# A two-layer hybrid decoder trunk: the instruction order found with the compiler's other model of time

## The chip, the cores and the metric

The kernel runs on one core of one Trainium2 chip. The metric is the device time of one execution in microseconds (us). The engines are TensorE (PE in the profile; its weight loads are PEld), VectorE (DVE), ScalarE (ACT), GpSimd (POOL) and SyncE (SP), which issues most of the DMAs. Each engine takes its own instructions strictly in the order in which they stand in its program and waits on semaphores for the others.

## The reference

Two layers of a decoder trunk on one sequence of S = 512 tokens and width D = 1024, all in fp32. The core of it, shortened:

```python
def hybrid_layer(x, ...):
    proj = rmsnorm(x, norm1_g) @ w_in            # 1024 -> 9568 columns, split among the branches
    y_ssd = ssd_mixer(ssd_z, ssd_xbc, ssd_dt, ...)        # Mamba-2: causal conv, chunked scan, gated norm
    y_mla = mla_mixer(mla_cq, mla_ckv, mla_kr, ...)       # 8 heads of latent attention, causal softmax
    y_gdn = gdn_mixer(gdn_qkv, gdn_z, gdn_b, gdn_a, ...)  # gated DeltaNet: causal conv, chunked recurrence
    mixed = g_ssd * (y_ssd @ w_ssd_out) + g_mla * (y_mla @ w_mla_out) + g_gdn * (y_gdn @ w_gdn_out)
    h = x + mixed @ w_out
    return h + square(relu(rmsnorm(h, norm2_g) @ w_up)) @ w_down     # 1024 -> 4096 -> 1024
```

In the chunked recurrences of the SSD and the DeltaNet (GDN) branch a state is carried from one chunk of tokens to the next. A final RMSNorm ends the trunk.

## The kernel before

The kernel is one long straight program without loops on the chip. Nearly all of its time is dense products on TensorE. An fp32 product is made of three matmuls on halves of the operands (`xh`, `xl` of the activations, `whi`, `wlo` of the weights), each with 512 columns as a rule:

```python
198    x = pe.matmul(o, ah, bh, start=start, stop=False, skip_group_check=more)
201    pe.matmul(o, ah, bl, start=False, stop=False, skip_group_check=more)
202    return pe.matmul(o, al, bh, start=False, stop=stop, skip_group_check=more)
```

The weights arrive by DMA as raw fp32 (`wraw`, `wr`), ScalarE casts the high half (L170) and VectorE subtracts to get the low half (L171). The results of dense products go to four PSUM banks (`acc`); a product can begin only when the bank of the fourth product before it has been read out. Three further banks (`sm`) and one more (`yt`) serve the small steps.

A layer runs in this order: front projection; latent attention (MLA, L590 to L711) in four pairs of heads `hp`; two SSD groups (L740 to L848); the triangular inverses for GDN; two GDN units `u` (`gdn_unit`, L1006 to L1137); the branch output projections (`out_proj`, L493), gates, `w_out`; then the feed-forward part. Each branch consists of chains of small steps that pass from engine to engine. The program writes them interleaved with dense products of the same or of the next branch, so that TensorE has something to do while VectorE and ScalarE work on a chain.

Three chains matter here.

- **A GDN chunk** (four chunks `t` of 128 tokens in each unit): TensorE L1057 and L1068, VectorE L1071 (four slices), TensorE L1074, VectorE L1079, ScalarE L1085 (four slices), TensorE L1088, VectorE L1097 (four slices: the new state `st`, which the next chunk's L1068 needs). Beside it the chunk's output: TensorE L1100 and L1107, ScalarE L1108, VectorE L1110, ScalarE L1116, VectorE L1122 and L1123, the inverse root of L278 (VectorE) and L279 (POOL), VectorE L1125 and L1128. L1108 writes the buffer `wk3`, of which there is one, so it waits for the L1128 of the chunk before. After the last chunk the transposes L1133 take the unit's output to `yt`, L274 (ScalarE) and L275 (VectorE) split it into `yh`, `yl`, and these are operands of `w_gdn_out`.
- **An MLA head**: scores on TensorE (L667 to L671) for four blocks of rows, VectorE L676 (mask and maximum), ScalarE L678 (exponential), VectorE L679 and L680, then transposes on TensorE (L688), whose results ScalarE (L270) and VectorE (L271) split, then the products with the values (L704 to L706).
- **A causal convolution** of a dense result (`conv_silu`, L720): ScalarE L725, then three times VectorE L729, which read the `acc` bank; L283 finishes the SiLU.

The order on each engine is not the order of the text. The tile framework builds the program from the text, with buffers from pools and semaphores between the engines, and a list scheduler inside it chooses at each step among the instructions that are ready, by a model of what each costs. The text steers it in two ways: `tc.high_priority()` marks steps as urgent, and `behind(key, ins)` (L153) ties a small step to stand behind a chosen dense product, by a dependency that sets the order only and puts no semaphore into the program:

```python
151    tc.add_manual_dep(i, o.name, order_only, reason="behind a product")
1085   act.activation(hv(vd)[:, h], hv(pw)[:, h], AF.Copy, scale=cd[:, t, h : h + 1])
1110   dve.scalar_tensor_tensor(hv(o)[:, h], hv(pq)[:, h], hdec(0, t, h), hv(o)[:, h], ALU.mult, ALU.add)
```

## Time and profile before

| what | value |
|---|---|
| time, median of 2 runs | 2269.6 us (2269.21 to 2269.99) |
| profiled execution, device time | 2269.02 us |
| its span in the profile | 2267.2 us |
| mean granted TensorE clock | 0.999 |
| TensorE (PE) busy | 2251.3 us, 99% |
| VectorE (DVE) busy | 1649.1 us, 73% |
| ScalarE (ACT) busy | 1185.1 us, 52% |
| GpSimd (POOL) busy | 64.6 us, 3% |
| moved by DMA | 244.07 MB, mean 108 GB/s |

The span is counted from the first to the last instruction of the profiled execution; about 2 us of device time lie outside it. "Busy" counts the time in which an engine has at least one instruction under way. Matmuls are pipelined: the row of one shows a longer duration than the step from its start to the start of the next.

### The profile page before, as it was taken

The page shows a single profiled execution, that of the slowest core. Times are in us where ns is not written, and L with a number is a line of the kernel's source. Part 1 is how long each engine was busy: PE and PEld are TensorE (multiplying, and loading weights), DVE is VectorE, ACT ScalarE, POOL GpSimd, SP SyncE. Part 2 cuts the span into 40 slices and gives each one's busy share as a digit, 9 for nine tenths or more (in the row PEclk, how much of TensorE's full clock was granted, in tenths as well). Part 3 has the DMA queues.
Part 4 walks back from the last instruction along what each step waited for, and adds up shares of the span by engine and source line. Part 5 has one row for each costly group of instructions (what it writes and reads, how often), then busy time and mean ns, then how long its engine had stood idle before and what let it go on. Part 6 is the DMA issues. An engine that isn't in the chain of part 4 may idle for free.

```text
span 2267.2 us, 32128 instructions
## 1 busy us (share of the span) xinstructions
PE 2251.3 (99%) x11758; PEld 1868.3 (82%) x11758; DVE 1649.1 (73%) x3315; ACT 1185.1 (52%) x2444; POOL 64.6 (3%) x84
## 2 busy tenths in 40 slices
PE   9999999999999999999999999999999999999998
PEld 8888888888888888888888878888888888888886
DVE  8886567776767778767868865668657668778668
ACT  6665744333443555554656657443345445645545
POOL 1000000000000000000010000000001000000000
PEclk9999999999999999999999999999999999999999
DMA  4223633442225143233132246335422251433231
GB/s 143 82 78 109 194 104 119 137 135 75 84 65 177 56 149 112 94 111 103 52 101 80 71 125 192 103 111 149 122 84 75 66 186 38 167 112 102 84 112 47
DMA packets 220030, 244.07 MB, mean 108 GB/s; under 512 B 34256, under 2 KB 172384, under 8 KB 219872
## 3 DMA queue, kind: packets, MB, share of 16 engines
q1 hardware_dynamic: 219872, 242.02, 34.7%
q8 instruction: 92, 1.51, 0.3%
q14 instruction: 66, 0.54, 0.1%
HBM read 225.53 MB, written 11.74 MB: 105 GB/s over the span
## 4 chain that ended last, share of the span: by engine, by line
PE 95%; DVE 3%; DMA 1%; ACT 1%; POOL 0%; issue 0%; SPq 0%; DVEq 0%; POOLq 0%; ACTq 0%
PE acc L198 24%; PE acc L202 24%; PE acc L201 24%; PE sm L201 3%; PE sm L198 3%; PE sm L202 3%; PE sm L688 1%; PE sm L792 1%; DVE wlo L171 1%; PE yt L704 1%; PE sm L1074 1%; PE sm L1100 1%; PE sm L803 1%; PE yt L201 1%; PE yt L198 1%; PE yt L202 1%
## 5 line engine op out<-in xcount | busy, mean ns | idle before, releaser
L171 DVE TENSOR_TENSOR wlo<-wraw,whi 128x512 fp32r<-128x512 f32 (+1 forms) x536 | 364.9, 686 | 331.9 <-ACT whi L170 321.8
L170 ACT CAST whi<-wraw 128x512 fp32r<-128x512 f32 (+1 forms) x536 | 329.3, 618 | 518.8 <-PE acc L201 345.7
L198 PE MATMUL acc<-xh,whi 128*128 128x512 f32 (+1 forms) x1344 | 525.3, 391 | 0.0
L202 PE MATMUL acc<-xh,wlo 128*128 128x512 f32 (+1 forms) x1344 | 520.6, 388 | 0.6 <-DVE wlo L171 0.6
L201 PE MATMUL acc<-xl,whi 128*128 128x512 f32 (+1 forms) x1344 | 519.2, 387 | 0.0
L202 PEld LDWEIGHTS acc<-xh,wlo 128*128 128x128 f32 x1344 | 252.5, 188 | 50.4 <-DVE wlo L171 1.4
L198 PEld LDWEIGHTS acc<-xh,whi 128*128 128x128 f32 x1344 | 252.5, 188 | 48.2 <-ACT xh L274 0.4
L201 PEld LDWEIGHTS acc<-xl,whi 128*128 128x128 f32 x1344 | 252.7, 188 | 47.6 <-DVE xl L275 0.7
L170 ACT CAST whi<-wr 128x512 fp32r<-128x512 f32 x168 | 104.4, 621 | 109.5 <-PE acc L201 47.3
L198 PE MATMUL acc<-yh,whi 128*128 128x512 f32 x384 | 152.1, 400 | 0.0
L201 PE MATMUL acc<-yl,whi 128*128 128x512 f32 x384 | 150.3, 391 | 0.0
L202 PE MATMUL acc<-yh,wlo 128*128 128x512 f32 x384 | 149.8, 390 | 0.0
L171 DVE TENSOR_TENSOR wlo<-wr,whi 128x512 fp32r<-128x512 f32 x168 | 113.0, 686 | 36.4 <-ACT whi L170 35.4
L729 DVE SCALAR_TENSOR_TENSOR ckl<-acc,pc,ckl 128x511 f32<-128x511 f32 (+2 forms) x168 | 121.2, 743 | 19.2 <-ACT ckl L725 10.9
L198 PEld LDWEIGHTS acc<-yh,whi 128*128 128x128 f32 x384 | 71.5, 188 | 16.5 <-ACT yh L274 2.3
L202 PEld LDWEIGHTS acc<-yh,wlo 128*128 128x128 f32 x384 | 72.1, 188 | 15.0
L201 PEld LDWEIGHTS acc<-yl,whi 128*128 128x128 f32 x384 | 72.1, 188 | 14.2
L198 PE MATMUL acc<-whi,xh 128*128 128x512 f32 (+1 forms) x208 | 79.9, 384 | 1.2 <-DVE ckl L729 1.2
L202 PE MATMUL acc<-whi,xl 128*128 128x512 f32 (+1 forms) x208 | 79.3, 381 | 0.0
L201 PE MATMUL acc<-wlo,xh 128*128 128x512 f32 (+1 forms) x208 | 79.2, 381 | 0.0
L488 ACT ACTIVATE eE<-eE,cum 128x128 f32<-128x128 f32 x192 | 62.5, 390 | 29.3 <-DMA eE<-d_c 24.5
L1220 DVE TENSOR_TENSOR h<-h,acc 128x512 f32<-128x512 f32 x120 | 76.9, 679 | 0.0
(468 smaller groups left out, 4498.7 us busy)
## 6 DMA issues: line engine op xcount, KB each, us to landing
wraw<-in_w_in_dram SPq DMA_DIRECT2D x144, 512.0 KB, 3.6
wraw<-in_w_up_dram SPq DMA_DIRECT2D x64, 512.0 KB, 3.6
wr<-in_w_down_dram SPq DMA_DIRECT2D x32, 1024.0 KB, 5.1
eE<-d_c SPq DMA_DIRECT2D x48, 256.0 KB, 4.3
wraw<-in_w_mla_out_dram SPq DMA_DIRECT2D x16, 512.0 KB, 3.3
eE<-d_e SPq DMA_DIRECT2D x32, 256.0 KB, 3.0
wraw<-in_w_ssd_out_dram SPq DMA_DIRECT2D x16, 512.0 KB, 3.3
wraw<-in_w_gdn_out_dram SPq DMA_DIRECT2D x16, 512.0 KB, 3.4
```

What stands on the lines that cost most here:

```text
L170: act.copy(hi, raw)
L171: dve.tensor_tensor(lo, raw, f32(hi), ALU.subtract)
L198: x = pe.matmul(o, ah, bh, start=start, stop=False, skip_group_check=more)
L201: pe.matmul(o, ah, bl, start=False, stop=False, skip_group_check=more)
L202: return pe.matmul(o, al, bh, start=False, stop=stop, skip_group_check=more)
L488: act.activation(o[:, i], o[:, i], AF.Relu, scale=-1.0, bias=cum[:, t, h0 + i : h0 + i + 1])
L688: pe.transpose(ps[:, n : n + P], pn[t][:, kb * P : (kb + 1) * P], ident)
L704: pe.matmul(o, v_h, th[:, c : c + w], start=kb == 0, stop=False)
L729: dve.scalar_tensor_tensor(acc[:, d:], ps[:, : S - d], taps_[3 - d], acc[:, d:], ALU.mult, ALU.add)
L792: x = pe.matmul(py[64 * i : 64 * i + 64, c * P : (c + 1) * P], xd[:, t, h * 64 : (h + 1) * 64], e2[h // 4][:, h % 4, :], start=True, stop= ...
L803: pe.matmul(po[:, c * P : (c + 1) * P], st[:, c * P : (c + 1) * P], ctl[:, tok], start=True, stop=True)
L1220: dve.tensor_tensor(hs_, hs_, ps[t], op)
```

## The change

One argument where the tile framework is opened. The function that computes, and with it every instruction, stays as it is.

```diff
-    with tile.TileContext(nc) as tc:
+    with tile.TileContext(nc, schedule_with_timeline_sim=True) as tc:
         hybrid_kernel(tc, args, out)
```

With it, the list scheduler asks another model of time what an instruction costs and when it would be ready, so it chooses another order on the engines. The buffers, the dependencies and the rules of `behind` and `high_priority` are the same. On TensorE about two rows in three stand at another place than before, the farthest more than 150 rows away; on VectorE most of the moves are within 30 rows, on SyncE within 17; GpSimd's order is the same. Three places show what moved. The names in the rows are the program's buffers with their numbers: `acc` and `sm` and `yt` are PSUM banks, `xh`/`xl`, `yh`/`yl`, `whi`/`wlo` the halves of operands; a row stands for one matmul or, with "x4", for four of the same names.

**The end of GDN unit u=1 in the first layer, on TensorE.** The rows of before, from the L1074 of chunk t=2 (`sm_1458`) to the transposes L1133 after the last chunk:

```order
L1074 MATMUL sm_1458_6831<-tok_1357_6346,tok_999_4501 128x128 x4
L198 MATMUL acc_1492_6972<-xh6_31_160,whi_1501_7025 128x512
...
L202 MATMUL acc_1505_7045<-yh0_1150_5419,wlo_1509_7050 128x512
L1088 MATMUL sm_1461_6843<-wk2_1460_6838,kt_1353_6332 128x256
...
L1107 MATMUL sm_1465_6857<-st_1444_6776,ft_1333_6230 128x256
L198 MATMUL acc_1505_7045<-yh1_1151_5420,whi_1508_7049 128x512
...
L1068 MATMUL sm_1475_6894<-st_1462_6846,ft_965_4342 128x256
...
L1074 MATMUL sm_1476_6901<-tok_1357_6346,tok_999_4501 128x128 x4
L198 MATMUL acc_1505_7045<-yh3_1153_5422,whi_1510_7065 128x512
...
L1100 MATMUL sm_1478_6908<-wk1_1477_6906,eE_1472_6886 128x128 x4
...
L1107 MATMUL sm_1480_6914<-st_1462_6846,ft_1333_6230 128x256
...
L1133 MATMUL yt_1487_6943<-ct_0_75,tok_1358_6347 128x128 x4
```

The rows of the change at the same place:

```order
L202 MATMUL acc_1522_7131<-xh7_32_161,wlo_1532_7185 128x512
L1074 MATMUL sm_1458_6831<-tok_1357_6346,tok_999_4501 128x128 x4
L1088 MATMUL sm_1461_6843<-wk2_1460_6838,kt_1353_6332 128x256
...
L1088 MATMUL sm_1461_6843<-wk2_1460_6838,kt_1354_6333 128x256
...
L1107 MATMUL sm_1465_6857<-st_1444_6776,ft_1333_6230 128x256
...
L1068 MATMUL sm_1475_6894<-st_1462_6846,ft_965_4342 128x256
L1074 MATMUL sm_1476_6901<-tok_1357_6346,tok_999_4501 128x128 x4
L1100 MATMUL sm_1478_6908<-wk1_1477_6906,eE_1472_6886 128x128 x4
...
L1107 MATMUL sm_1480_6914<-st_1462_6846,ft_1333_6230 128x256
L1133 MATMUL yt_1487_6943<-ct_0_75,tok_1358_6347 128x128 x2
L198 MATMUL acc_1505_7045<-yh4_1154_5423,whi_1513_7083 128x512
```

Before, 60 dense matmuls (L198, L201, L202 on `acc_1492`, `acc_1505`, `acc_1506`, `acc_1521`, `acc_1522`) stand between the first row and the L1133; in the change there is none, the rows of the chain follow one another, and those dense products stand ahead of it or behind. The second layer has the same picture.

**The end of GDN unit u=0, on VectorE.** Before, from the L1097 that makes the last state (`st_1303`) to the convolutions of `acc_1377` and `acc_1378`, whose banks a later dense product waits for:

```order
L1097 SCALAR_TENSOR_TENSOR st_1303_6104<-st_1285_6034,dec_254_1091,sm_1302_6101 128x128 x4
...
L1071 SCALAR_TENSOR_TENSOR tok_1198_5604<-sm_1316_6152,ndec_255_1093,tok_1198_5604 128x128 x4
L283 SCALAR_TENSOR_TENSOR ft_1332_6229<-ft_1332_6229,ckl0_1346_6301 128x512
...
L729 SCALAR_TENSOR_TENSOR ckl0_1372_6419<-acc_1359_6348,pc_13_122,ckl0_1372_6419 128x511
...
L729 SCALAR_TENSOR_TENSOR ckl0_1372_6419<-acc_1359_6348,pc_13_122,ckl0_1372_6419 128x510
...
L1110 SCALAR_TENSOR_TENSOR wk3_1320_6171<-sm_1321_6172,dec_254_1091,wk3_1320_6171 128x128 x2
...
L1037 TENSOR_TENSOR tok_1357_6346<-sm_1373_6426,gork_996_4493 128x4x128
...
L729 SCALAR_TENSOR_TENSOR ckl0_1390_6517<-acc_1377_6446,pc_13_122,ckl0_1390_6517 128x511
L275 SCALAR_TENSOR_TENSOR yl0_1158_5427<-yt_1328_6201,pc_13_122,yh0_1150_5419 128x512
...
L729 SCALAR_TENSOR_TENSOR ckl0_1390_6517<-acc_1377_6446,pc_13_122,ckl0_1390_6517 128x509
```

The rows of the change:

```order
L1097 SCALAR_TENSOR_TENSOR st_1303_6104<-st_1285_6034,dec_254_1091,sm_1302_6101 128x128 x4
L1110 SCALAR_TENSOR_TENSOR wk3_1305_6114<-sm_1306_6115,dec_254_1091,wk3_1305_6114 128x128 x4
L1071 SCALAR_TENSOR_TENSOR tok_1198_5604<-sm_1316_6152,ndec_255_1093,tok_1198_5604 128x128 x4
L283 SCALAR_TENSOR_TENSOR ft_1332_6229<-ft_1332_6229,ckl0_1346_6301 128x512
...
L729 SCALAR_TENSOR_TENSOR ckl0_1372_6419<-acc_1359_6348,pc_13_122,ckl0_1372_6419 128x511
L729 SCALAR_TENSOR_TENSOR ckl1_1375_6433<-acc_1360_6349,pc_13_122,ckl1_1375_6433 128x511
...
L1110 SCALAR_TENSOR_TENSOR wk3_1320_6171<-sm_1321_6172,dec_254_1091,wk3_1320_6171 128x128 x4
L729 SCALAR_TENSOR_TENSOR ckl0_1390_6517<-acc_1377_6446,pc_13_122,ckl0_1390_6517 128x511
...
L729 SCALAR_TENSOR_TENSOR ckl1_1393_6531<-acc_1378_6447,pc_13_122,ckl1_1393_6531 128x511
...
L729 SCALAR_TENSOR_TENSOR ckl0_1390_6517<-acc_1377_6446,pc_13_122,ckl0_1390_6517 128x509
...
L1037 TENSOR_TENSOR tok_1357_6346<-sm_1373_6426,gork_996_4493 128x4x128
```

The L1097, L1110, L1071 of the last two chunks and the L729 of four convolutions now stand close together, without the weight splits (L171) that were between them. On TensorE the chain from the L1088 of `sm_1302` to the L1107 of `sm_1321` has 40 dense matmuls in it before and none in the change.

**The last MLA head of the first layer (hp=3), on TensorE.** Before, from the last score matmul (`sm_527`) over the transposes L688 to the products with the values (`yt_531`):

```order
L671 MATMUL sm_527_2132<-kph_121_571,qpl1_148_688 128x512
L688 MATMUL sm_532_2146<-ct_0_75,pn0_517_2100 128x128
L198 MATMUL acc_564_2287<-xh3_28_157,whi_568_2306 128x512
L201 MATMUL acc_564_2287<-xl3_36_165,whi_568_2306 128x512
L688 MATMUL sm_532_2146<-ct_0_75,pn1_521_2113 128x128
...
L688 MATMUL sm_532_2146<-ct_0_75,pn3_529_2139 128x128
...
L201 MATMUL acc_564_2287<-xl4_37_166,whi_571_2324 128x512
L704 MATMUL yt_531_2145<-mix_533_2151,cqh1_483_1955 128x512
L202 MATMUL acc_564_2287<-xh4_29_158,wlo_572_2325 128x512
...
L705 MATMUL yt_531_2145<-mix_534_2152,cqh1_483_1955 128x512
...
L202 MATMUL acc_564_2287<-xh5_30_159,wlo_572_2325 128x512
```

The rows of the change:

```order
L671 MATMUL sm_527_2132<-kph_121_571,qpl1_148_688 128x512
L688 MATMUL sm_532_2146<-ct_0_75,pn0_517_2100 128x128
...
L688 MATMUL sm_532_2146<-ct_0_75,pn3_529_2139 128x128
...
L688 MATMUL sm_538_2169<-ct_0_75,pn3_529_2139 128x128
L704 MATMUL yt_531_2145<-mix_533_2151,cqh1_483_1955 128x512
L705 MATMUL yt_531_2145<-mix_534_2152,cqh1_483_1955 128x512
...
L706 MATMUL yt_531_2145<-pt0_145_683,cql1_484_1956 128x256
L764 MATMUL sm_576_2363<-ct_0_75,tok_542_2190 128x128 x4
L764 MATMUL sm_578_2377<-ct_0_75,tok_542_2190 128x128 x4
L198 MATMUL acc_607_2556<-xh0_25_154,whi_610_2560 128x512
```

Before, dense matmuls of the SSD projections (`acc_563`, `acc_564`) stand among the transposes and the value products; in the change none do, and right behind the L764 transposes comes `acc_607`, whose bank is that of `acc_579`.

## The prediction

> **What bounds the kernel now.** I read the page's busy times first, then the chain that ended last, then TensorE's waits and its groups by shape.
>
> ```profile
> PE 2251.3 (99%) x11758; PEld 1868.3 (82%) x11758; DVE 1649.1 (73%) x3315; ACT 1185.1 (52%) x2444; POOL 64.6 (3%) x84
> PE 95%; DVE 3%; DMA 1%; ACT 1%; POOL 0%; issue 0%; SPq 0%; DVEq 0%; POOLq 0%; ACTq 0%
> PE sm L1068 <- ACT wk L1108: 1.2, 2, 0.6
> PE acc L198 <- DVE ckl L729: 1.2, 2, 0.6
> ```
>
> TensorE is busy for 2251.3 of 2267.2 us, the chain runs on it for 95% of the span, and its longest wait in the middle of the program is 0.6 us (waits: us in total, times, longest). Of the 15.9 us without a matmul about 9 lie after the last one and 1 at the head. So every other engine's time counts only where TensorE has to wait for it, and an order can only win what waiting is left.
>
> Some waiting hides in the busy time, because a matmul that is issued late shows as a longer row:
>
> ```profile
> L198 PE MATMUL acc<-xh,whi 128*128 128x512 f32 x1280 | 507.6, 397 | 0.0
> L202 PE MATMUL acc<-xh,wlo 128*128 128x512 f32 x1280 | 502.8, 393 | 0.6 <-DVE wlo L171 0.6
> L201 PE MATMUL acc<-xl,whi 128*128 128x512 f32 x1280 | 501.1, 391 | 0.0
> L198 PE MATMUL sm<-xh,whi 128*128 128x512 f32 x176 | 68.5, 389 | 0.0
> L198 PE MATMUL acc<-yh,whi 128*128 128x512 f32 x384 | 152.1, 400 | 0.0
> ```
>
> The undisturbed group has 389 ns. The excess is (8 + 4 + 2) x 1280 = 18 us, and for the L198 with `yh` 11 x 384 = 4 us. With the 6 us of listed waits and a few us in smaller groups, **about 30 us of waiting are in the kernel**, all that an ideal order could win. A gain of more than 2% (45 us, about what a measurement of this kernel can tell from no change) is then not to be had.
>
> **The change part by part.** No instruction is added or removed, so TensorE's work is the same and only waiting can differ. The order decides where the dense matmuls stand, and the question for each chain is how many stand inside it. I price each place as the length of the chain minus TensorE's own work in it.
>
> *(a) The end of GDN unit u=1.* Before, this stretch of the first layer costs nothing:
>
> ```profile
> 674.90:696.60 21.70, 21.70 (x118) 18.74 (x117) 15.74 (x54) 8.86 (x29) 3.02 (x3) 1.00 0.18 49
> 674.92 1.05 PE L1074 MATMUL sm<-tok,tok 128*128 128x128 f32 x8
> 676.01 0.69 DVE L1079 TENSOR_TENSOR wk<-sm,gcc 128x512 f32<-128x512 f32 x1
> 676.73 0.88 ACT L1085 ACTIVATE wk<-sm,gcd 128x128 f32<-128x128 f32 x3 [1.02 <-DVE wk L1079]
> 678.01 0.38 ACT L1085 ACTIVATE wk<-sm,gcd 128x128 f32<-128x128 f32 x1
> 679.89 1.11 DVE L1097 SCALAR_TENSOR_TENSOR st<-st,dec,sm 128x128 f32<-128x128 f32 x4
> 680.92 1.12 DVE L1110 SCALAR_TENSOR_TENSOR wk<-sm,dec,wk 128x128 f32<-128x128 f32 x4
> 683.75 1.12 DVE L1071 SCALAR_TENSOR_TENSOR tok<-sm,ndec,tok 128x128 f32<-128x128 f32 x4
> 686.88 1.05 PE L1100 MATMUL sm<-wk,eE 128*128 128x128 f32 x8
> 687.76 1.03 PE L1107 MATMUL sm<-st,ft 128*128 128x256 f32 x4
> 688.12 0.58 ACT L1108 COPY wk<-sm 128x512 f32<-128x512 f32 x1 [3.63 <-DVE tok L1128]
> 688.44 0.58 PE L198 MATMUL acc<-yh,whi 128*128 128x512 f32 x1
> 691.12 0.16 DVE L1122 TENSOR_TENSOR gms<-gos,grt 128x4 f32<-128x4 f32 x1 [0.20 <-ACT gk L1116]
> 691.76 1.01 POOL L279 TENSOR_TENSOR gms<-gms,nhalf 128x4 f32<-128x4 f32 x1 [5.12 <-DVE gms L278]
> 693.00 1.14 DVE L1128 SCALAR_TENSOR_TENSOR tok<-tok,gms,wk 128x128 f32<-128x128 f32 x4
> L1061 DVE TENSOR_TENSOR gk<-sm,ct 128x256 f32<-128x256 f32 x16 | 6.7, 416 | 0.0
> L1063 DVE TENSOR_TENSOR eE<-eE,gk 128x512 f32<-128x512 f32 x16 | 11.0, 687 | 0.0
> L1116 ACT ACTIVATE gk<-wk 128x128 f32<-128x128 f32 x64 | 19.1, 299 | 6.7 <-DVE wk L1110 6.5
> L274 ACT ACTIVATE yh<-yt,pc 128x512 fp32r<-128x512 f32 x16 | 11.0, 687 | 11.6 <-PE yt L1133 11.5
> ```
>
> The window has TensorE at 21.70 of 21.70 us (first pair of numbers; the 1.00 is the granted clock), since 60 dense matmuls stand in the chain and beside it. In the change none does. Then the chain from the end of the first L1074 runs at its own speed: L1079 0.69, L1085 1.26, the L1088 and L1100 behind them about 0.95 more, L1097 1.11, L1110 1.12 and L1071 1.12 in VectorE's order; then L1061, L1063 and two rows of 0.16 like L1122 (1.4), beside which the last L1074 runs; L1079 0.69, L278 0.17, L279 on POOL 1.01 with 0.2 of hand-over, L1125 0.16, L1128 1.14: 11.0 us. L1108 needs the one `wk3` that this L1128 reads (its row above names that wait), so the last chunk's output starts only now: L1108 0.58, L1110 1.12, the last L1116 0.5, L1122 to L278 0.5, L279 1.2, L1125 0.16, L1128 1.14: 5.2. With hand-overs 16.4 us until L1133. TensorE's work in it, by steps from start to start: eight of 128 columns take 0.88 (L1100 to L1107), 0.11 each, four of 256 columns 0.68 (L1107 to the L198), 0.17 each. An fp32 instruction counts two. L1074, L1100 twice and L1057 are 28 of the former, L1088, L1107 twice and L1068 are 16 of the latter: 3.1 + 2.7 = 5.8. The stall is 16.4 - 5.8 = 10.6 us, about 6 of it in one piece between the last L1107 and the L1133. Then comes `acc_1505` on `yh4`, which needs L1133 and ScalarE's 0.7 us L274, for four tiles in turn, partly covered: 2 us. So **12.5 us per layer, 25 in all**.
>
> *(b) The end of unit u=0.* The change has no dense matmul in the chain here either, and VectorE runs late with the convolutions.
>
> ```profile
> L729 DVE SCALAR_TENSOR_TENSOR ckl<-acc,pc,ckl 128x511 f32<-128x511 f32 (+2 forms) x168 | 121.2, 743 | 19.2 <-ACT ckl L725 10.9
> L283 DVE SCALAR_TENSOR_TENSOR ft<-ft,ckl 128x512 f32<-128x512 f32 x36 | 24.5, 686 | 1.7 <-ACT ft L282 1.3
> ```
>
> From the L1097 of `st_1303` to the L729 that frees the bank of `acc_1377` VectorE holds 10 to 12 L729 of 0.743 (8.2), five runs of four slices (L1097, L1110 twice, L1071, L1128: 5.6), four L283 (2.7), L1061, L1063, L1079 (1.8) and small rows (1.2): 19.5 us. TensorE has about 12.3 us until `acc_1397`, which needs that bank: the chain's 5.8, the 24 matmuls of `acc_1395` and `acc_1396` at 0.227, and 1 of transposes. The stall is **7.2 us per layer, 14 in all**.
>
> *(c) MLA.* Per head, the last score block needs L676 to L680 before its L688 can run, and the L688 need L270 and L271 before L704 and L705:
>
> ```profile
> L676 DVE CUSTOM_DVE_ANT_0 pn<-sm,causal,qrs 128x512 f32<-128x512 f32 x16 | 11.9, 743 | 0.6 <-PE sm L671 0.5
> L678 ACT ACTIVATE pn<-pn,mx 128x512 f32<-128x512 f32 x16 | 11.5, 720 | 1.1 <-DVE mx L676 0.9
> L679 DVE RECIPROCAL sme<-sme 128x1 f32<-128x1 f32 x64 | 10.1, 158 | 0.9 <-ACT pn L678 0.7
> L680 DVE TENSOR_SCALAR pn<-pn,sme 128x512 f32<-128x512 f32 x16 | 7.8, 485 | 0.4
> L271 DVE TENSOR_TENSOR mix<-sm,mix 128x512 fp32r<-128x512 f32 x16 | 11.0, 690 | 6.3 <-ACT mix L270 6.1
> L766 DVE TENSOR_TENSOR tok<-sm,dtq 128x512 f32<-128x512 f32 x16 | 10.4, 683 | 0.3 <-PE sm L764 0.3
> ```
>
> L676 0.74, L678 0.72, L679 0.16, L680 0.49 and an estimated 0.3 for the read-outs of the accumulators between them are 2.4; the L688 of the earlier blocks cover a few tenths: 2.2. L704 and L705 wait another 0.9, the rest of the L270 and L271 that the other transposes don't cover. 3.1 for each of the last two heads, in which the change has no dense matmul: 6.2. Then `acc_607` waits for the bank of `acc_579`: behind the last L706, L270 0.6, L271 0.69, two L766 1.37 and four L729 2.97 are 5.6, less 0.9 of transposes on TensorE, and L270 starts a little before the last L706: 4. Two us more for the earlier heads, which lose some of their matmuls. **12 us per layer, 24 in all.**
>
> *(d) What goes.* The waits that are there now, about 30 us, are replaced by those above at the same places, and in the SSD stage and the feed-forward part the change keeps two or more dense matmuls between small steps. I count them as gone: **-30 us**. Bounds: 0, if each stays, and -30.
>
> *(e) The clock.* The trace shows once what an idle TensorE does to it, at the end:
>
> ```profile
> 2258.00:2260.00 2.00, 0.24 (x2) 0.00 (x0) 1.81 (x5) 0.32 (x1) 0.01 (x1) 1.00 0.74 285
> 2260.00:2262.00 2.00, 0.00 (x0) 0.00 (x0) 1.43 (x3) 0.40 (x2) 0.54 (x1) 1.00 0.28 109
> 2262.00:2264.00 2.00, 0.00 (x0) 0.00 (x0) 1.24 (x4) 0.00 (x0) 0.55 (x1) 0.56 0.68 262
> 0.99 7.56 PE L352 MATMUL yt<-cosT 128*128 128x128 f32 x44 [0.99 <-POOL cosT L109]
> ```
>
> The last matmul ends at 2258.24; the granted clock is 1.00 up to 2262 and 0.56 on average in the two us behind: it halves 4.0 us after the last matmul. The 6 us piece of (a) is longer. The price of coming back is not in the trace; nearest is the first row of the program, 44 matmuls of 172 ns where the eight of L1100 take 0.88 us, 110 each: 2.7 us more. Between 0 and 2.7 per layer I take 2.5, as near to that row: **+5**.
>
> [...]
>
> *SyncE.* Two of the first weight loads are issued after some small loads, but they wait for buffers until about 10 us in both orders: 0. For the rest, weights are loaded and split further ahead than TensorE uses them (L171 costs it 0.6 us in all), and moves of 17 rows don't use that up.
>
> **The sum:** 25 + 14 + 24 - 30 + 5 = +38 us on the profiled 2269.0, which is 0.6 below the median of the runs: **2307 us, slower by 1.7%**.
>
> **Rivals.**
> - *The bare chains cost more (slower by over 2%).* The durations above are those of undisturbed steps. If VectorE is late at the start of each chain by one split (L171 0.69) per step, or the waits of (d) stay at their places, 10 to 30 us come on top: 2317 to 2340. For it: VectorE is 73% busy, and in (b) it is the bound. Against it: the change's rows put the splits ahead of the chains. 0.36.
> - *The chains are covered after all (faster than before).* The mechanism: the dense matmuls that the change puts ahead of a chain put TensorE behind VectorE there, so that the chain's steps are ready when TensorE arrives, and only the -30 us of (d) acts. It decides if the stalls of (a) to (c) together stay under 30 us, half of their 63. Time 2245 to 2267, for example 2255 with 15 us of stalls left. Against it: in (a) each step needs the one before it, so nothing can be ready ahead. 0.10.
> - *No effect.* Stalls of about 30 us that replace the 30 of before: 2267 to 2280. 0.10.
> - *My forecast*, 2280 to 2316: 0.44.
>
> **Range and chances.** Low end: half of (a) to (c) gone gives 2275, and a part of the case of no effect lies below that, so 2270; high end: none of the 30 us of (d) goes and VectorE is late besides, 2345. That leaves 0.10 out below and 0.08 above. Faster by over 2% needs 45 us, more than all waiting: 0.01. Slower by over 2% (above 2315) is the first rival and the edge of the forecast: 0.39. Within 2%: 0.60.
>
> **What would show it.** In the profile of the changed kernel the waits of TensorE should list L1133 after L1128 with two waits of 5 to 6 us, L1068, L1074 and L1100 of GDN with 1 to 3 us each, `acc` L198 after L729 with some 7 us in two of them, and L688 after L680 with some 2 us; TensorE's busy time should fall by about the hidden 25 us. A granted clock under 1.00 in the window behind the L1133 shows (e). The excess of the L198 `acc<-xh,whi` group over 389 ns should shrink. The prediction is wrong if TensorE's listed waits stay under 20 us, if the stalls stand at other places than these three, or if weights arrive late (L201 or L202 waiting for L170, L171 or a DMA).

## The result, and the profile after

The change makes the kernel slower: 2370.9 us, median of two runs (2370.32 and 2371.51), against 2269.6; ratio 1.0444, 95% interval 1.0427 to 1.0461. The profiled execution took 2370.32 us, its span is 2368.5: 101.3 us more than before. The prediction had the direction; its 2307 us and its range up to 2345 are too low.

The busy times on the page of the changed kernel:

```profile
PE 2283.0 (96%) x11758; PEld 1898.6 (80%) x11758; DVE 1650.5 (70%) x3315; ACT 1177.8 (50%) x2444; POOL 68.5 (3%) x84
```

The counts are those of before. TensorE idles for 2368.5 - 2283.0 = 85.5 us, before 15.9: **69.6 us more idle**. And the same number of matmuls, 11758, kept it busy for **31.7 us more**. These are two different losses, and they add up to the 101.3.

The first is in TensorE's list of waits (us in total, times, longest), which has 76.1 us in all and had 6.3:

```profile
PE yt L1133 <- DVE tok L1128: 10.1, 2, 5.1
PE acc L198 <- DVE ckl L729: 9.7, 3, 4.6
PE sm L754 <- DVE ft L283: 7.7, 2, 4.2
PE sm L688 <- DVE pn L680: 7.5, 6, 2.2
PE acc L198 <- DVE cql L271: 7.2, 2, 3.6
PE acc L198 <- DVE vl L271: 4.9, 4, 2.2
PE sm L1100 <- DVE gms L1123: 4.8, 2, 2.4
PE sm L974 <- issue: 3.3, 2, 1.8
PE sm L1088 <- ACT wk L1085: 3.1, 2, 1.6
PE sm L1100 <- DVE wk L1079: 2.5, 2, 1.2
PE acc L198 <- DVE ql L619: 2.3, 2, 1.1
PE sm L1074 <- DVE tok L1071: 1.8, 4, 0.4
```

Nearly every wait comes twice, once a layer: the same places stall in both layers.

The second is the clock. Windows of the changed kernel (us, TensorE's busy time and matmuls, weight loads, VectorE, ScalarE, GpSimd, then the granted clock, the DMAs' share and GB/s): the end of GDN unit u=0 with a stretch that follows it at full clock, then the end of unit u=1, then an MLA head.

```profile
657.60:661.00 3.40, 0.99 (x10) 0.89 (x9) 3.40 (x9) 2.30 (x4) 0.00 (x0) 1.00 0.01 2
661.00:671.30 10.30, 10.30 (x35) 8.89 (x34) 9.18 (x25) 4.06 (x13) 3.02 (x2) 0.50 0.09 26
674.00:684.00 10.00, 10.00 (x61) 8.69 (x60) 7.92 (x19) 5.42 (x9) 1.38 (x1) 1.00 0.09 15
...
743.80:748.90 5.10, 0.05 (x1) 0.05 (x1) 2.58 (x12) 1.86 (x9) 1.01 (x1) 0.75 0.00 0
746.40:753.20 6.80, 3.57 (x10) 2.71 (x11) 2.81 (x10) 1.51 (x4) 1.01 (x1) 0.50 0.00 0
...
207.00:210.50 3.50, 1.43 (x9) 0.98 (x7) 2.51 (x8) 1.39 (x4) 0.00 (x0) 1.00 0.27 53
210.50:213.90 3.40, 3.29 (x10) 2.44 (x11) 1.76 (x4) 1.45 (x3) 0.00 (x0) 0.50 0.69 254
```

After a stall of only 2.4 us the clock stands at 0.50 for 10.3 us, with TensorE busy all the time: 35 matmuls, where a stretch at full clock has 61. In the whole execution the trace's clock record has fourteen such stretches ahead of the last matmul, 71.7 us, in which TensorE was busy for 60.7. At a granted clock of 0.50 half of that, 30.4 us, is counted as lost, an estimate that explains the 31.7 us of busy time but for 1.3. Dense matmuls of 512 columns start 0.427 us apart in these stretches (86 steps) and 0.227 at full clock; by these steps the loss would be 28.4 us. So 69.6 idle + 30.4 clock + 1.3 = 101.3.

### The profile page after: what moved, and what is told of

It is laid out like the page before. It is cut to its first block, busy times and chain, and to the rows that moved or that the text cites. A ratio compares the mean times of both kernels' runs of the same rounds, so it can differ in the third digit from the quotient of the medians.

```text
span 2368.5 us, 32159 instructions
## 1 busy us (share of the span) xinstructions
PE 2283.0 (96%) x11758; PEld 1898.6 (80%) x11758; DVE 1650.5 (70%) x3315; ACT 1177.8 (50%) x2444; POOL 68.5 (3%) x84
## 5 line engine op out<-in xcount | busy, mean ns | idle before, releaser
L171 DVE TENSOR_TENSOR wlo<-wraw,whi 128x512 fp32r<-128x512 f32 (+1 forms) x536 | 366.0, 687 | 386.5 <-ACT whi L170 376.9
L170 ACT CAST whi<-wraw 128x512 fp32r<-128x512 f32 (+1 forms) x536 | 329.6, 618 | 554.3 <-PE acc L201 359.0
L198 PE MATMUL acc<-xh,whi 128*128 128x512 f32 (+1 forms) x1344 | 529.5, 396 | 15.8 <-DVE ckl L729 8.6
L201 PE MATMUL acc<-xl,whi 128*128 128x512 f32 (+1 forms) x1344 | 524.1, 391 | 0.0
L202 PE MATMUL acc<-xh,wlo 128*128 128x512 f32 (+1 forms) x1344 | 522.4, 392 | 0.0
L198 PEld LDWEIGHTS acc<-xh,whi 128*128 128x128 f32 x1344 | 255.8, 191 | 67.5 <-ACT tok L282 9.0
L202 PEld LDWEIGHTS acc<-xh,wlo 128*128 128x128 f32 x1344 | 256.0, 191 | 51.9 <-DVE wlo L171 0.8
L201 PEld LDWEIGHTS acc<-xl,whi 128*128 128x128 f32 x1344 | 256.7, 191 | 50.2 <-issue 1.0
L170 ACT CAST whi<-wr 128x512 fp32r<-128x512 f32 x168 | 104.3, 621 | 104.3 <-PE acc L201 45.3
L198 PE MATMUL acc<-yh,whi 128*128 128x512 f32 x384 | 152.4, 401 | 2.2 <-ACT yh L274 1.6
L201 PE MATMUL acc<-yl,whi 128*128 128x512 f32 x384 | 152.2, 396 | 0.1
L202 PE MATMUL acc<-yh,wlo 128*128 128x512 f32 x384 | 149.7, 392 | 0.0
L171 DVE TENSOR_TENSOR wlo<-wr,whi 128x512 fp32r<-128x512 f32 x168 | 114.7, 689 | 33.9 <-ACT whi L170 32.8
L729 DVE SCALAR_TENSOR_TENSOR ckl<-acc,pc,ckl 128x511 f32<-128x511 f32 (+2 forms) x168 | 121.5, 744 | 12.5 <-ACT ckl L727 6.0
L488 ACT ACTIVATE eE<-eE,cum 128x128 f32<-128x128 f32 x192 | 61.6, 393 | 58.7 <-DMA eE<-d_c 54.1
L198 PEld LDWEIGHTS acc<-yh,whi 128*128 128x128 f32 x384 | 72.4, 190 | 20.2 <-ACT yh L274 3.3
L201 PEld LDWEIGHTS acc<-yl,whi 128*128 128x128 f32 x384 | 72.8, 190 | 16.3 <-DVE yl L275 1.0
L202 PEld LDWEIGHTS acc<-yh,wlo 128*128 128x128 f32 x384 | 72.8, 190 | 14.7
L201 PE MATMUL acc<-wlo,xh 128*128 128x512 f32 (+1 forms) x208 | 80.1, 386 | 0.0
L202 PE MATMUL acc<-whi,xl 128*128 128x512 f32 (+1 forms) x208 | 79.6, 387 | 0.0
L198 PE MATMUL acc<-whi,xh 128*128 128x512 f32 (+1 forms) x208 | 74.2, 390 | 1.1 <-DVE ckl L729 1.1
```

The source lines that it names most:

```text
L170: act.copy(hi, raw)
L171: dve.tensor_tensor(lo, raw, f32(hi), ALU.subtract)
L488: act.activation(o[:, i], o[:, i], AF.Relu, scale=-1.0, bias=cum[:, t, h0 + i : h0 + i + 1])
L729: dve.scalar_tensor_tensor(acc[:, d:], ps[:, : S - d], taps_[3 - d], acc[:, d:], ALU.mult, ALU.add)
```

## The experiments

The order on an engine can be held without any other edit: after the program is traced, each instruction gets an order-only dependency on the one that shall stand ahead of it, from a table of the order of before (or of the change). The instructions stay the same.

```python
for a, b in zip(seg, seg[1:]):
    tc.add_manual_dep(ins[b], ins[a].name, only, reason="pinned order")
```

The tables of each kernel are named below; what isn't in a table is ordered by the other model (in the second experiment: by that of before). The scheduler makes this order anew around the one that is held, so an engine that isn't in a table has neither the order of the change nor that of before. Going by the rows of the traces (line and names), 83% of VectorE's rows in the second experiment stand in the change's order and 77% in that of before; TensorE's, where only VectorE and ScalarE are held, agree to 83% with either. The runs therefore don't cross the orders of the two kernels; they show what a held order makes of the time when the rest adapts to it. Rows of a kernel with added lines are named here by the lines of the kernel before.

**TensorE's order of before held** (table: PE of before).

> The changed kernel, with TensorE's order of before held by order-only dependencies; VectorE, ScalarE and SyncE keep the order that the other model gives them. Theory (TensorE's order alone makes the loss: the 78 us of longer idle pieces and the 30 us of half clock come from chains without dense matmuls in them): 2265 to 2285 us, listed waits of TensorE under 15 us, no half clock before the last matmul. Rival (the order on VectorE and ScalarE does a part of it, splits in the wrong place): 2300 to 2350 us, with waits on L171 or L729 listed.

2343.6 us, ratio 1.0323 (1.0293 to 1.0353). The theory fell: with TensorE's own order of before 74 us of the 101 stay. The time is in the rival's range, but the waits that the rival named are not what fills it: L171 has 0.9 us, L729 none. Half clock before the last matmul is less and not gone, six stretches with 11.1 us lost. The waits are at other places:

```profile
PE yt L824 <- DVE wk L823: 14.4, 9, 3.7
PE sm L764 <- DVE tok L283: 8.8, 10, 1.3
PE sm L877 <- DVE ft L283: 7.7, 3, 3.6
```

These are steps of the SSD stage and of the GDN matrices for which TensorE waited 1.3 us at most in either of the two kernels. An order of TensorE that is good with one order on VectorE and ScalarE is bad with another.

**TensorE's order of the change held, in the kernel before** (table: PE of the change).

> The kernel before, with the changed kernel's TensorE order held; the other engines are ordered by the model of before. Theory (TensorE's order alone): 2355 to 2385 us, with the same stalls at L1133, L754, L688 and the same stretches of half clock. Rival (VectorE and ScalarE matter too): under 2340 us.

2378.3 us, ratio 1.0475 (1.0445 to 1.0506). The time is as the theory had it: with TensorE's order of the change the kernel is as slow under the old model as under the new one; 7 us more are within what executions of one such kernel differ by (the last experiment). The stalls are only in part the same: L1133 has 10.3 us and L688 7.7, but L754 is not in the list, and L1100 has 16.4 where the change has 7.3 (at the end of unit u=0 6.7 us in one piece, 2.4 in the change).

**Two and three engines held** (tables of before: PE and ACT; PE and DVE; PE, DVE and ACT; DVE and ACT).

> The changed kernel with TensorE's and ScalarE's order of before held; VectorE and SyncE by the other model. With TensorE alone held (2343.6 us) TensorE waited 14.4 us for L824 and 7.7 for L877, and before one such L824 ScalarE sat on L488 until the DMA of eE landed, with L821 queued behind it. Theory S (ScalarE's order does this): 2275 to 2300 us, and the L824 waits gone. Theory V (VectorE's order does it): 2320 to 2345 us.

> The changed kernel with TensorE's and VectorE's order of before held; ScalarE and SyncE by the other model. Theory S: 2320 to 2345 us, L824 still waited for. Theory V: 2275 to 2300 us.

> The changed kernel with the order of before held on TensorE, VectorE and ScalarE; only SyncE is ordered by the other model. If the order on the three engines that compute holds all of the difference: 2268 to 2274 us. If SyncE's order of the DMA issues has a part (the loads of eE by L486 among the loads of weights): 2280 to 2330 us, with waits on the DMA of eE or of wraw.

> The changed kernel with VectorE's and ScalarE's order of before held, TensorE's left to the other model. If TensorE's order is what matters first: 2340 to 2380 us, with the long idle pieces at the ends of the chains still there. If TensorE's order is harmless once the other two are right: under 2300 us.

| order of before held on | time, us | against before |
|---|---|---|
| nothing (the change) | 2370.9 | 1.0444 |
| PE | 2343.6 | 1.0323 |
| PE, ACT | 2316.0 | 1.0201 (1.0172 to 1.0231) |
| PE, DVE | 2326.6 | 1.0248 (1.0218 to 1.0278) |
| PE, DVE, ACT | 2270.1 | 0.9999 (0.9988 to 1.0010) |
| DVE, ACT | 2412.4 | 1.0626 (1.0595 to 1.0657) |

Neither theory S nor theory V holds alone. The time with VectorE is in the range of theory S and L824 is still waited for (8.4 us); with ScalarE the waits of L824 shrink from 14.4 to 3.8 us, but the time is 16 us above that theory's range, with L877 still at 8.2. Either engine brings a part back beside TensorE, 28 and 17 us, and both together all 74. SyncE's order of the transfers has no part: with the other three engines held, it is the other model's, and the time is that of before. Without TensorE, the order of before on VectorE and ScalarE makes it slower than anything else, 2412.4 us, above both of the ranges expected. The long pieces at the ends of the chains, which were expected to stay, are mostly gone (L1133 has 2.1 us); other waits took their place:

```profile
PE acc L198 <- ACT whi L170: 37.2, 34, 3.7
PE acc L202 <- DVE wlo L171: 15.0, 17, 2.2
```

TensorE, ordered by the other model, asks for the weights of its dense products at other moments than those at which ScalarE casts (L170) and VectorE subtracts (L171) them. The order of this program is one plan for all its engines. By these runs TensorE's order of the change is enough to make the loss, its order of before is not enough to take it away, and all three orders together are.

**TensorE's order of before held in some stages only** (slices of the table: front and MLA; the two GDN units; and at last both with slices for DVE and ACT too).

> The changed kernel with TensorE's order of before held only in the front projection and the MLA stage of both layers. In these stages the changed kernel has about 34 us of idle pieces more and 12 us lost to half clock. Theory (the stalls of a stage are its own and add up): 2371 - 45 = 2326 us, 2318 to 2336. Rival (what is gained in one stage is waited for in the next, since VectorE is late there anyway): 2345 to 2371 us.

> The changed kernel with TensorE's order of before held only in the two GDN units of both layers. There the changed kernel has 24 us of idle pieces more and some 11 us lost to half clock. Theory (they add up): 2371 - 36 = 2335 us, 2327 to 2345. By the prediction's own prices (25 + 14 of stalls, 5 of clock, and the small waits back) it would be 2371 - 30 = 2341. Rival (the stall moves to the output projection behind): 2355 to 2371 us.

> The changed kernel with the order of before held on TensorE, VectorE and ScalarE, but only in the front and MLA stages and in the GDN units of both layers; the SSD stage, the inverses and all that follows stay with the other model. Theory (each stage's stalls are its own once all three engines agree): 2371 - 45 - 36 = 2290 us, 2280 to 2300, what is left being the waits at L754 and L974 and their half clock (about 18 us). Rival (the seams between the held and the free stages make new waits, as with TensorE alone held in the SSD stage): 2305 to 2340 us.

2341.4 (1.0313, 1.0283 to 1.0343), 2337.1 (1.0294, 1.0264 to 1.0324) and 2295.9 us (1.0114, 1.0094 to 1.0135). In the GDN units TensorE's order alone gives back 34 us (36 expected from their stalls and half clock; the 30 by the prediction's prices are not ruled out). In MLA it gives 30 of 45, which lies between the theory's range and the rival's: idle time is 26.3 us less and the loss at half clock 7.9 less, but TensorE's busy time falls by 0.8 us only, so some 7 us come back inside its rows. With three engines the two stages together give 75, as the sum of stage losses (81) had it within the clock's scatter. What is left, 26 us, is for the most part two places that the held slices don't cover, with 10.4 us of waits in the third kernel, and 10.9 us lost at half clock:

```profile
PE sm L754 <- DVE ft L283: 6.7, 2, 4.0
PE sm L975 <- issue: 2.0, 1, 2.0
PE sm L974 <- issue: 1.7, 1, 1.7
```

**Idle matmuls in the stalls** (tables of the change on PE, DVE and ACT, with matmuls of no use added).

```diff
+                fl = fill(9, po) if u == 0 and t == T - 1 else None      # ahead of the last L1100 of unit 0
+                        fl = fill(20, ps)                                # ahead of the first L1133 of unit 1
+            fl = fill(13, ps) if g else None                             # ahead of the L754 of SSD group 1
```

> The changed kernel with its own order held on TensorE, VectorE and ScalarE, and idle matmuls of no use put into three of its stalls per layer: 13 ahead of the L754 of the second SSD group, 9 ahead of the last L100 step (L1100) of GDN unit 0, 20 ahead of the L1133 of unit 1 (its first two transposes move behind them). They compute nothing that is used. Each fits into the wait that is there, so without the clock nothing changes. Theory (the half clock after an idle stretch is a cost of its own): the half-clock stretches behind these six places vanish, and with them 14.8 us of TensorE's work lost in them: 2353 to 2360 us. Rival (the half clock costs nothing more, it lies in waits anyway): 2368 to 2373 us.

2361.1 us (2360.24 to 2363.97), ratio 1.0404 (1.0386 to 1.0421), against 1.0444: about 10 us less time with 84 matmuls more. In the profiled execution TensorE's idle time is 18.9 us less, the added matmuls make about 20.1 us of work, and the loss at half clock is 9.8 us less. The rival is out; the size is under the 14.8 expected, and the median 1 us above the theory's range. Around the L1100 of the first layer:

```profile
656.00:661.00 5.00, 4.56 (x26) 3.64 (x25) 4.75 (x17) 3.36 (x13) 0.00 (x0) 1.00 0.51 159
661.00:671.30 10.30, 10.05 (x58) 8.45 (x56) 10.30 (x28) 5.64 (x16) 3.63 (x2) 1.00 0.08 26
```

58 matmuls in the 10.3 us, where the change had 35. The half clock is gone behind five of the six places; behind the sixth, the L1100 of the second layer, a wait of 2.8 us of the dense products for a bank that L729 reads (1.1 in the change) brings one step of it back. This is the bank wait of the prediction's part (b), which the slow TensorE of the change had hidden in part; in the first layer it does not show in either. And three short stretches appeared where the change has none. TensorE's work lost at half clock fell from 30.4 to 20.6 us.

**Ties at the end of GDN unit u=1.** Six dense products per layer are issued behind steps of the chain, by the kernel's own `behind` and `place`:

```diff
+    HELD = {("y", 0, 0, 0): ("pw", 2), ("y", 0, 1, 0): ("pq", 2), ("y", 0, 1, 1): ("pk", 3), ("y", 0, 3, 0): ("pw", 3),
+            ("y", 0, 3, 1): ("pq", 3), ("g", 1, 0, 0): ("pq", 3)}
...
-                    end = mm3(..., k0 + k == 0, k0 + k == last)
+                    end = mm3(..., k0 + k == 0, k0 + k == last, key=tied(tag, k0 + k, j))
...
+                    place(("gdn", ly, "pw", t), x)        # and "pk", "pq" likewise, in unit 1
```

> The changed kernel with six dense products per layer (of the gates and of w_gdn_out) tied behind steps of the chain at the end of GDN unit 1, so that dense matmuls stand in that chain again. Theory (that place costs 9.4 us of idle pieces and about 2 of half clock per layer, and the products taken from their early places are not missed there): 2371 - 22 = 2349 us, 2343 to 2354. Rival (they were covering waits at their early places, so these open): 2355 to 2371 us.

2353.3 us, ratio 1.0367 (1.0346 to 1.0388): 17.6 us less; the median is inside the theory's range, one of the two runs 0.9 us above it. The 5.06 us at L1133 is gone from both layers, and so is the half clock behind it; waits of 1.6 us for L1088 and 0.5 for L1074 stay. No new wait over 0.6 us is listed, so the products had been spent on places that did not need them. The gain is idle time, 15.0 us in the profiled execution; the loss at half clock is only 2.2 us less in all, as new stretches appear elsewhere.

**One pair of exponentials later on ScalarE.** The L754 wait was not priced in the prediction. The timeline of the change shows what is queued ahead of it (start, length; what ended the idle time before, in brackets):

```profile
314.63 1.28 ACT L488 ACTIVATE eE<-eE,cum 128x128 f32<-128x128 f32 x4 [1.32 <-DMA eE<-d_c]
...
317.89 1.28 ACT L488 ACTIVATE eE<-eE,cum 128x128 f32<-128x128 f32 x4 [1.84 <-DMA eE<-d_c]
...
320.10 0.62 ACT L282 ACTIVATE ft<-ckl 128x512 f32<-128x512 f32 x1
...
320.84 0.68 DVE L283 SCALAR_TENSOR_TENSOR ft<-ft,ckl 128x512 f32<-128x512 f32 x1
...
321.67 0.66 PE L754 MATMUL sm<-ct,ft 128*128 128x128 f32 x2 [4.24 <-DVE ft L283]
```

ScalarE sits on two L488 until the transfers of `eE` land, and the L282 that the L754 needs stands behind them. Two other rows lie between the last of these L488 and the L282; in the kernel before it is seven, with five casts among them. The edit puts them behind the copy L757:

```diff
-                    seg_exp(e2[q], t, h0 + 4 * q)
+                    seg_exp(e2[q], t, h0 + 4 * q, kt_copy if g and t == 1 else None)
```

> The changed kernel with one pair of steps per layer moved on ScalarE: the L488 of the second SSD group's chunk t=1, which wait for the DMA of eE, stand behind L757 instead of ahead of the L282 on which the L754 of that group waits in the end. The order of all the other engines is the changed kernel's but for four lines. Theory (ScalarE, stopped by a transfer that lands later than the other model has it, makes the 7.7 us of L754 and the half clock behind it, 3.9 us): 2371 - 11.6 = 2359 us, 2355 to 2363, and L754 gone from the list of waits. Rival (VectorE is late there anyway, or the exponentials are then missed by L787 and L792): 2366 to 2373 us.

The wait is gone: L754 has 0.7 us in all, and ScalarE's idle time on the DMA of `eE` falls from 54.1 to 30.9 us (with the other waits of these rows from 58.6 to 50.9). But the median is 2367.0 us (four runs, 2364.24 to 2376.01; ratio 1.0442, 1.0420 to 1.0465), which is no difference from the change that can be measured, and lies above the theory's range and, by its number alone, in the rival's. The mechanism is shown; its worth is not. The times follow the clock: the runs with a mean granted clock of 0.984 and 0.983 took 2364.7 and 2364.2, that with 0.981 took 2369.3, that with 0.980 took 2376.0. In the profiled one TensorE's work lost at half clock was 32.9 us, more than the change's 30.4, with one stall less per layer; its idle time is 6.9 us less.

No version beat the kernel before; the best is the one with its order on three engines, which is the same in time.

## Why the prediction was wrong

- **That chains without dense matmuls stall (parts a to c): right.** Stalls of 58 us were measured at these places' waits against 63 predicted; that the sums are so near is partly luck, since the parts miss both ways. (a) 18.8 (L1133 10.1, L1088 3.1, L1100 2.5, L1074 0.9, `yh` and L507 2.2) for 25; the piece ahead of L1133 was 5.1 for 6. (b) 6.8 for 14: the bank wait was 1.1 us in one layer and none in the other, where 7 each had been counted. That the half clock slowed TensorE down so much that VectorE's convolutions were done in time is supported by the run with idle matmuls in one layer only. (c) 18.0 for the last two heads and the bank behind them (L688 7.5, L704 and L705 1.9, about half of it at an earlier head, L729 8.6) for 20, but 14.4 for the earlier heads, for which it had 4: there dense products wait for banks that the splits of the values and queries empty late (`vl`, `cql` L271, `ql` L619).
- **Places not priced: 11 us.** L754, where ScalarE's queue is held up by a transfer, and L974 in the inverse (7 us more are small waits at the start and elsewhere). The prediction looked for dense matmuls in chains, on TensorE and VectorE; it never went through ScalarE's order for instructions that wait on a DMA. Its sentence on SyncE holds.
- **(d), 30 us of small waits that go: wrong, this step failed.** The 6.3 us of listed waits went into the longer list, and 1.3 us of busy time that the clock does not explain came on top: -5.0 for -30. Busy time was expected to fall by 25 and rose by 31.7, of which the clock explains 30.4 by the estimate above. The group whose excess over 389 ns should shrink went from 397 to 402 ns, and is at 397 as before in the rows outside the half-clock stretches:

```profile
L198 PE MATMUL acc<-xh,whi 128*128 128x512 f32 x1280 | 513.4, 402 | 15.8 <-DVE ckl L729 8.6 <-DVE cql L271 7.2
```

  What failed is the reading that longer rows are waiting. In the trace of before, 256 dense matmuls of 512 columns stand right behind a small step. 226 of them take 460 ns or more, and together the 256 hold 22.8 us of excess over 389 ns, most of the 30. 223 of the 256 wait for no semaphore at all, so no other engine holds them up. Of the 7856 behind another dense matmul, 22 are as long. An example in the kernel before, with the weight loads (PEld), right behind an L1107:

```profile
688.42 0.19 PEld L198 LDWEIGHTS acc<-yh,whi 128*128 128x128 f32 x1
688.44 0.58 PE L198 MATMUL acc<-yh,whi 128*128 128x512 f32 x1
688.63 0.19 PEld L201 LDWEIGHTS acc<-yl,whi 128*128 128x128 f32 x1
688.86 0.39 PE L201 MATMUL acc<-yl,whi 128*128 128x512 f32 x1
```

  The weight load of the long row starts 0.02 us ahead of it, that of the next row 0.23 us. So it is with all 256: the 226 long ones have their weight load less than 0.05 us ahead, the other 30 at least 0.16. In this trace the excess goes with the switch from a small step to a dense product, in 226 of 256 cases, and with a wait for another engine in 33 at most. Why the weight load starts late there is not shown. TensorE's busy time without what half clock took shows the same: 2251.3 us before, 2252.6 in the change, and not under 2249.5 in any of the fourteen profiled kernels. The bounds given for (d) were 0 and -30, and the taken value was the end that no row supported.
- **(e), the clock: failed as much, 5 us for 30.4.** It took from the tail of the trace that TensorE must be idle for 4.0 us in one piece, and so counted one place per layer. The trace of the change shows half clock after single waits of 2.2 and 2.4 us. In all traces of this study the half-clock stretches begin, within one execution, on one grid of 3.413 us, and those ahead of the last matmul last whole steps of it (3.41, 6.83 or 10.24 us in the change). Over thirteen profiled executions of changed or held kernels, the ends of the programs included, a grid step at full clock in which TensorE was busy under 40% of the time was followed by half clock 76 times out of 76; with 40 to 50% 28 of 39, with 50 to 60% 15 of 73, above that 12 of 8543. In the trace of the change alone, ahead of its last matmul, it was 10 of 10, 1 of 2, 2 of 9 and 1 of 648. So in these executions half clock goes with the share of one step in which TensorE was idle and not with the length of the gap alone: a gap of 2.2 us, most of it in one step, with TensorE busy for 1.36 of 3.41 us, was enough.
- **The first rival (slower by over 2%, 0.36) has the direction, but its 2317 to 2340 us are too low as well.** Of its two conditions, VectorE late by a split per step did not come, and the 25 us of (d) that stay did, though not as waits. What it lacks is the clock and the places not priced. The "covered after all" rival and the "no effect" rival are out.
- **Of what it would show:** L1133 behind L1128 with two waits of 5 us, L688 behind L680 with 2.2 and L1100 with 1.2 and 2.4 stood in the list as announced. `acc` L198 behind L729 had 4.6 and 4.0, but at the bank of part (c); the two waits of 7 announced for (b) did not come, and L1068 is not in the list. Stalls at other places than the three were named as a sign of being wrong, and there are some, L754 above all. Weights were not late in the change; they were when only VectorE and ScalarE were held.

With the measured terms the prediction's sum is 76.1 of waits - 6.3 of before + 30.4 of clock + 1.3 = 101.5. Against its 38 that is 25.4 for (e), 25.0 for (d), 18 for places not priced, and 5 less for (a) to (c).

What stays open: why the other model spends the dense products early and puts the L488 ahead of L282. No run here shows what it believes of the costs; that it takes the transfer of `eE` to land sooner than it does fits the order but is only argued. No run pairs the exact orders of the two kernels on different engines either.

## What to carry to other kernels

In this kernel, with TensorE busy for 99% of the span, the order of the instructions was itself the tuned part, and one plan for all engines: held on VectorE and ScalarE alone it cost 41.5 us more than the change. Before an order is exchanged, go through it for three things: chains in which no dense matmul stands, instructions that wait on a transfer with others queued behind them on their engine (here two L488, which waited 1.3 and 1.8 us ahead of the L282), and gaps of 2 us and more on TensorE: behind waits of 2.2 and 2.4 us half clock followed here, and the fourteen stretches of it lost 30.4 us by the estimate above, 2.2 us each. Ties that hold dense work back for the end of a chain took a few lines and were worth 18 us here. And before longer rows are counted as waiting that an order could win, look at what they stand behind: here they were the first dense matmuls behind small steps.

## What was not expected of the hardware

In the changed kernel the half-clock stretches ahead of the last matmul begin at these times, which lie on one grid (us from the span's start, and length):

```
149.04 3.41   210.48 3.41   230.96 3.41   319.71 6.83   548.40 3.41   661.04 10.24   746.38 6.83
1319.82 6.83  1394.91 3.41  1405.15 6.83  1497.31 3.41  1722.59 3.41  1835.23 3.41   1920.56 6.83
```

All differences are whole multiples of 3.4133 us (210.48 - 149.04 is 18 of them, 1920.56 - 149.04 is 519). The same stall was followed by half clock in one layer and not in the other. The wait of 2.18 us ahead of the first L688 of the last two heads stands in both layers of the changed kernel; the grid steps in which it lies have these busy times:

```profile
207.07:210.48 3.41, 1.36 (x9) 0.94 (x7) 2.43 (x7) 1.32 (x3) 0.00 (x0) 1.00 0.27 52
...
1381.25:1384.67 3.42, 1.82 (x11) 1.31 (x9) 2.47 (x9) 1.78 (x5) 0.00 (x0) 1.00 0.18 16
1384.67:1388.08 3.41, 2.37 (x12) 1.73 (x13) 2.11 (x5) 1.35 (x3) 0.00 (x0) 1.00 0.84 291
```

In the first layer most of it lies in one step, TensorE is busy for 1.36 of 3.41 us there, and half clock follows. In the second it is split between two steps, and the clock stays at 1.00 behind both.

Executions of one kernel, the last experiment's, differ by up to 12 us (2364.24 to 2376.01), while the kernel before, which has no half clock ahead of its last matmul, stayed within 2 us over all its runs. From the span's start the grid lies at 2.3 us in the trace of the change and at 2.6 in that of before. Whether it moves between executions of one kernel, and whether that makes the 12 us, is not shown: only one execution of each kernel has a trace.
